# Re-ordering the first stage of a two-block network on one Trainium2 core: operands ahead of squares, eight un-normed blocks in two PSUM groups, modulation weights moved behind the layer norm

## The chip, the core and the metric

The program runs on one core of one Trainium2 chip. The metric is the device time of one execution in microseconds (us). The engines of the core run side by side, each working through its own queue in order: TensorE (PE, matmuls; PEld its weight loads), VectorE (DVE), ScalarE (ACT), GpSimd (POOL) and SyncE (SP), which here only issues transfers from memory. An instruction waits at the head of its engine's queue until what it needs is there, and everything behind it on that engine waits too.

## What is computed

The input x is 512 tokens by 1024 features, in float32. Two network blocks follow each other. The part that the change touches is the first half of the first block:

```python
h = rmsnorm(x, norm1_g)
z = h @ w_in + b_in                       # 1024 -> 6656 columns, 52 blocks of 128
z_glu, z_rx, z_rg, z_ga, z_gb = split(z)
u = z_glu[..., :1024] * sigmoid(z_glu[..., 1024:])
u = causal_depthwise_conv(u, conv_dw_w, conv_dw_b)      # 31 taps
u = silu(layernorm(u, conv_ln_g, conv_ln_b))
y_a = u @ conv_w_out + conv_b_out
xb = causal_depthwise_conv(z_rx, lru_conv_w, lru_conv_b)   # 4 taps
hb = rg_lru(xb, ...)                      # gates of 80 x 80 blocks, a linear recurrence over time
y_b = (hb * gelu(z_rg)) @ lru_w_out
m = sigmoid(z_ga) * y_a + sigmoid(z_gb) * y_b
x = x + m @ w_mix_out
x = x + (silu(h @ ffn_w1) * (h @ ffn_w3)) @ ffn_w2      # h: a second rmsnorm
...
mods = silu(c) @ w_ada + b_ada            # 9 x 1024 numbers, used from the second block on
```

The second block has a feed-forward net, a token mixer (gated linear attention and forgetting attention, merged through w_out) and another feed-forward net; each takes scales and shifts from mods.

## The kernel before

Activations lie transposed: 128 features on the partitions, 512 tokens along the free dimension, so a 1024-wide activation is 8 tiles. A product with a weight block of 1024 x 128 is 8 slices of 128 x 128. For accuracy every operand is split into a rounded high part and a low rest (hi by ScalarE, lo = source - hi by VectorE or GpSimd), and `mm3` (L131 to L134) makes three matmuls of a slice: lines 132, 133, 134. A block of 8 slices is therefore 24 matmuls of 512 columns.

The program is a list of steps. A step has the weight tiles it needs and a function that is called when they are ready. One loop at the end of `build` walks the list, keeps weight transfers and splits (`prep_one`) running ahead, and spends what is left of a step's time, by its own table of costs in us, on a background queue `bg` (`runbg`); `defer(n, f)` calls f some steps later. The calls only name the instructions and their dependences; a scheduler then fixes the order on each engine, and `tc.issue_after(ins)` adds the wish that an instruction stand behind `ins` on its engine.

Staging: a weight tile lands in one of 5 buffers `st`, and its parts go to one of 5 `whi` and 5 `wlo`. Products accumulate in PSUM in one of 3 buffers `mm`; 5 others, `ax`, hold statistics, broadcasts and the convolution's accumulators. A product can begin only when a buffer of its group has been emptied by VectorE or ScalarE.

The order of the work of the first block:

- **Start** (`start_tiles`, L346). For each of the 8 tiles of x: hi and lo of x times the norm's weight g, and the square for the norm's sum. The norm's factor R is not waited for: the first seven blocks (`g0` is two, then `r0` to `r4`) multiply x g, not yet normed, and their results are multiplied by R when they are read (`raw_z`, L391). R takes a column sum over the partitions (ax L196), a square root by Newton steps on VectorE, and a broadcast (dg L217, ax L224).
- **Normed tiles** (`norm_h`, L368): h with R, split, during the un-normed steps. The convolution taps of the un-normed steps wait in the list `late` and are released after the last of these tiles.
- **First stage**, a list of short names (L590): `g` makes a gated unit and queues its 31 convolution taps (VectorE, L406, two accumulators in `ax` in turns, the first tap of each on ScalarE, L401 to L404); `r` makes a tile of z_rx with its 4 taps xb; `a` and `b` are gates, `s` the recurrence, `q` a gelu block times the recurrence, split into hbh and hbl.
- **y_b steps** (`yb_step`, L607): a sigmoid block (thb) and a product of 10 slices over hb.
- **Gate steps** (`ga_step`, L667), then the layer norm of the convolution's output has to be complete (`ln_push`, L651: mean, variance, 1/std, silu and split into u2h and u2l; its sum over tiles, lnm L479, is made by GpSimd), then **y_a steps** (`ya_step`, L676) use it.
- `ada_step` (L316) puts one 128-row piece of w_ada into the list: a transfer of 512 KB and one VectorE product with a sum (L327). 72 of them are spread over the steps: in the y_b steps (every second), the gate steps, six of the y_a steps, and further behind, in w_mix_out, the feed-forward net (`ada_between`: 1.0 a step) and ffn_w2.

`NKEEP` says of which weights tiles may be kept split when a second pass over the tokens' halves reads them again.

## Time and profile before

| | us |
|---|---|
| three runs | 2270.66, 2270.68, 2271.85 (median 2270.68) |
| the profiled execution | 2268.78 |
| its span on the core | 2267.1 |
| TensorE busy in the span | 2207.7 (97%) |
| VectorE busy | 1401.8 (62%) |
| ScalarE busy | 941.8 (42%) |
| GpSimd busy | 159.3 (7%) |

The profiled execution is some 1.7 us longer than its span, which runs from the first to the last instruction. Busy shares are means over stages that differ: in the first 340 us VectorE is busy nearly all the time, later about half. Matmuls are pipelined and overlap, so a matmul's duration in a row (0.4 us for 512 columns) is longer than the distance to the next. An idle piece is shown in brackets behind the instruction that ended it, with what it waited for.

### The profile page before, as it was taken

To read this page: it belongs to the slowest core of one execution; us is meant where nothing else is said; L and a number is where in the kernel's file an instruction comes from. 1 tells how busy PE (TensorE), PEld (TensorE's weight loads), DVE (VectorE), ACT (ScalarE), POOL (GpSimd) and SP (SyncE) were. 2 spreads that over 40 slices of the span, in tenths; PEclk is the share of its full clock that TensorE was granted. 3 is DMA by queue.
4 is the path that set the end of the run, shared out by engine and by line. 5 is a ranking of instruction groups with operands and counts; after the bars stand their busy time and mean duration, and the time that the engine had idled before them with its cause. 6 is when DMAs were issued, how large, how long until landed. Compare 5 with 4: busy or idle time off the path is not lost.

```text
span 2267.1 us, 29984 instructions
## 1 busy us (share of the span) xinstructions
PE 2207.7 (97%) x11688; PEld 1888.2 (83%) x11688; DVE 1401.8 (62%) x2349; ACT 941.8 (42%) x1517; POOL 159.3 (7%) x179
## 2 busy tenths in 40 slices
PE   8899999699999999999999999999999999999997
PEld 6687788588888899988889987888888899988887
DVE  7999996768555448433325768675656558433334
...
GB/s 191 118 92 122 101 134 225 82 144 174 203 195 192 150 103 149 131 94 102 86 102 129 161 96 57 66 47 103 66 75 75 117 89 96 147 95 98 92 121 66
DMA packets 81438, 265.54 MB, mean 117 GB/s; under 512 B 10208, under 2 KB 12512, under 8 KB 81296
## 3 DMA queue, kind: packets, MB, share of 16 engines
...
## 4 chain that ended last, share of the span: by engine, by line
PE 81%; DVE 11%; issue 1%; ACT 1%; DMA 0%; POOL 0%; DVEq 0%; ACTq 0%; POOLq 0%
PE mm L132 24%; PE mm L133 24%; PE mm L134 24%; DVE ax L406 3%; DVE wlo L126 1%; PE ax L1231 1%; PE ax L1232 1%; PE ax L1233 1%; PE ax L1286 1%; PE ax L224 1%; PE ax L1415 1%; DVE xb L406 1%; PE ax L196 1%; DVE xb L567 1%; DMA st<-w_ada 0%
## 5 line engine op out<-in xcount | busy, mean ns | idle before, releaser
L125 ACT ACTIVATE whi<-st 128x1024 fp32r<-128x1024 f32 (+3 forms) x420 | 427.1, 1018 | 959.3 <-PE mm L133 594.4
L126 DVE TENSOR_TENSOR wlo<-st,whi 128x1024 fp32r<-128x1024 f32 (+3 forms) x378 | 454.1, 1202 | 415.8 <-ACT whi L125 414.7
L132 PE MATMUL mm<-pfh,whi 128*128 128x512 f32 (+1 forms) x1676 | 568.9, 339 | 0.5 <-ACT sq L251 0.5
L133 PE MATMUL mm<-pfl,whi 128*128 128x512 f32 (+1 forms) x1676 | 565.6, 338 | 0.0
L134 PE MATMUL mm<-pfh,wlo 128*128 128x512 f32 (+1 forms) x1676 | 564.4, 337 | 1.2 <-DVE wlo L126 1.2
L134 PEld LDWEIGHTS mm<-pfh,wlo 128*128 128x128 f32 x1676 | 316.8, 189 | 34.0 <-DVE wlo L126 1.9
L132 PEld LDWEIGHTS mm<-pfh,whi 128*128 128x128 f32 x1676 | 317.2, 189 | 33.5 <-ACT sq L251 1.4
L133 PEld LDWEIGHTS mm<-pfl,whi 128*128 128x128 f32 x1676 | 317.1, 189 | 31.7 <-issue 0.5
L132 PE MATMUL mm<-hi,whi 128*128 128x512 f32 x464 | 183.0, 394 | 10.4 <-ACT hi L354 6.2
L133 PE MATMUL mm<-lo,whi 128*128 128x512 f32 x464 | 183.4, 395 | 1.3 <-DVE lo L355 1.3
L134 PE MATMUL mm<-hi,wlo 128*128 128x512 f32 x464 | 182.4, 393 | 0.4 <-DVE wlo L126 0.4
L132 PE MATMUL mm<-mh,whi 128*128 128x256 f32 (+1 forms) x528 | 176.7, 335 | 2.2 <-ACT mh L852 1.1
L133 PE MATMUL mm<-ml,whi 128*128 128x256 f32 (+1 forms) x528 | 176.9, 336 | 0.0
L134 PE MATMUL mm<-mh,wlo 128*128 128x256 f32 (+1 forms) x528 | 176.4, 334 | 0.0
L406 DVE SCALAR_TENSOR_TENSOR ax<-th,d_hdw,ax 128x508 f32<-128x508 f32 (+27 forms) x232 | 157.7, 729 | 1.1 <-ACT ax L401 0.2
L133 PE MATMUL mm<-m1l,whi 128*128 128x512 f32 x368 | 143.3, 390 | 0.2 <-DVE m1l L686 0.2
L134 PE MATMUL mm<-m1h,wlo 128*128 128x512 f32 x368 | 143.0, 389 | 0.0
L132 PE MATMUL mm<-m1h,whi 128*128 128x512 f32 x368 | 143.0, 389 | 0.0
L327 DVE SCALAR_TENSOR_TENSOR st<-st,crow 128x1024 f32<-128x1024 f32 x72 | 88.5, 1229 | 73.6 <-DMA st<-w_ada 73.5
L865 DVE TENSOR_TENSOR fs<-fs,mm 128x512 f32<-128x512 f32 (+1 forms) x75 | 45.0, 600 | 128.0 <-PE mm L134 127.7
L132 PEld LDWEIGHTS mm<-hi,whi 128*128 128x128 f32 x464 | 88.1, 190 | 29.6 <-ACT hi L354 6.2
L132 PEld LDWEIGHTS mm<-mh,whi 128*128 128x128 f32 x528 | 100.1, 190 | 13.1 <-ACT mh L852 1.5
...
## 6 DMA issues: line engine op xcount, KB each, us to landing
st<-w_gu SPq DMA_DIRECT2D x102, 512.0 KB, 3.5
st<-w_ada SPq DMA_DIRECT2D x72, 512.0 KB, 4.0
st<-ffn_w SPq DMA_DIRECT2D x56, 512.0 KB, 3.6
st<-w_in SPq DMA_DIRECT2D x51, 512.0 KB, 4.0
st<-w2fm SPq DMA_DIRECT2D x51, 512.0 KB, 3.5
...
st<-w_dn SPq DMA_DIRECT2D x24, 512.0 KB, 3.6
st<-w2v SPq DMA_DIRECT2D x16, 512.0 KB, 3.5
```

Source lines behind the costliest of these rows:

```text
L125: h = act(hi, src, AF.Copy)
L126: (eng or V).tensor_tensor(lo, src, hi, ALU.subtract)
L132: mm(out, whi, xh, start=start, stop=False)
L133: mm(out, whi, xl, start=False, stop=False)
L134: block[0] = mm(out, wlo, xh, start=False, stop=stop)
L196: mm(pc[:, i * nt + j:i * nt + j + 1], acc[:, r[0] + P * j:r[0] + P * (j + 1)], ones1, start=True, stop=True)
L224: mm(R[:, :nt * P], ones, dg.rearrange("p n t -> p (n t)"), start=True, stop=True)
L327: V.scalar_tensor_tensor(w, w, 1.0, crow, ALU.mult, ALU.mult, accum_out=mods[:, n:n + 1])
L406: V.scalar_tensor_tensor(acc[:, d:], u[:, :T - d], w, acc[:, d:], ALU.mult, ALU.add)
L567: V.tensor_tensor_scan(XB[j], GT[0, j], XB[j], 0.0, ALU.mult, ALU.add)
L865: V.tensor_tensor(s, s, rs(st["u"], r), ALU.mult)
L1231: mm(o, h[:, sl], hi[c], start=k == 0, stop=False)
```

## The change

1. **Start.** hi and lo of all eight tiles are made first; the squares follow. The weight tiles of the first four blocks are split at fixed places between them. w_ada and everything else at the start stay where they were.
2. **Un-normed blocks.** `r5` joins them: eight blocks instead of seven. The second, fourth and sixth take an `ax` buffer.
3. **Late list.** After the last normed tile only the first three entries of `late` are released (before: all); the rest, among them the first convolution, is released at the end of the un-normed steps, behind the last of their VectorE reads.
4. **Order wishes.** The first taps and totals of a convolution on ScalarE, and the high parts of xb and hb, are to stand behind the last emptying of a PSUM buffer (`EV`); taps on VectorE behind the last but one of its products (`DV`). The convolution's total overwrites its input instead of a new tile, and the last hb is split one step sooner.
5. **w_ada.** The y_b and gate steps carry none; all eight y_a steps carry one; the feed-forward net takes 1.2 a step; ffn_w2 the rest.
6. **Layer norm.** It is queued one background gap sooner, and the y_b and gate steps spend 1.15 times their rest on the background queue.
7. **NKEEP**: 8 of w_out instead of 3, none of w_mix_out instead of 3.

First place: TensorE's queue from the gate blocks to the y_a blocks (`mm` blocks over hi/lo of h are gate blocks, `ax` rows with ones are column sums, with dg broadcasts, `u2h` is the layer norm's result). Before:

```order
L132 MATMUL mm_3254<-hi_435,whi_3165 128x512
L133 MATMUL mm_3254<-lo_436,whi_3165 128x512
L134 MATMUL mm_3254<-hi_435,wlo_3166 128x512
L196 MATMUL ax_3281<-ones,lnm_1595 128x1 x4
L224 MATMUL ax_3290<-dg_3288,ones 128x512
L196 MATMUL ax_3326<-ones,lnv_3292 128x1 x4
L224 MATMUL ax_3348<-dg_3346,ones 128x512
L132 MATMUL mm_3404<-u2h_3352,whi_3205 128x512
```

With the change:

```order
L134 MATMUL mm_3089<-hi_435,wlo_2961 128x512
L196 MATMUL ax_3116<-ones,lnm_1563 128x1 x4
L132 MATMUL mm_3152<-hi_421,whi_2964 128x512
L133 MATMUL mm_3152<-lo_422,whi_2964 128x512
L134 MATMUL mm_3152<-hi_421,wlo_2965 128x512
L132 MATMUL mm_3152<-hi_423,whi_2964 128x512
L133 MATMUL mm_3152<-lo_424,whi_2964 128x512
L134 MATMUL mm_3152<-hi_423,wlo_2965 128x512
L132 MATMUL mm_3152<-hi_425,whi_2964 128x512
L224 MATMUL ax_3125<-dg_3123,ones 128x512
```

The sums for the mean stood behind the last gate block, and sums and broadcasts of the layer norm without a product between them; now they stand behind the fourth of eight gate blocks, with seven matmuls of the fifth between the sums and the broadcast. The other two steps of the norm have 54 matmuls between this broadcast and the sums of the variance (`lnv`), and 13 between those and their broadcast.

Second place: VectorE's queue at the end of the convolutions (`cv` and `th` with `ax`: a convolution's total; `st,mods`: a w_ada product; `s`, `dg`: the mean). Before:

```order
L327 SCALAR_TENSOR_TENSOR st_3245,mods<-st_3245,crow 128x1024
L126 TENSOR_TENSOR wlo_3206<-st_3129,whi_3205 128x1024
L327 SCALAR_TENSOR_TENSOR st_3303,mods<-st_3303,crow 128x1024
L126 TENSOR_TENSOR wlo_3249<-st_3169,whi_3248 128x1024
L327 SCALAR_TENSOR_TENSOR st_3437,mods<-st_3437,crow 128x1024
L126 TENSOR_TENSOR wlo_3399<-st_3209,whi_3398 128x1024
L327 SCALAR_TENSOR_TENSOR st_3479,mods<-st_3479,crow 128x1024
L126 TENSOR_TENSOR wlo_3441<-st_3252,whi_3440 128x1024
L447 TENSOR_TENSOR cv_3241<-cv_3241,ax_2949 128x512
L634 TENSOR_SCALAR s_3286<-ax_3281 128x4
L217 TENSOR_TENSOR dg_3288<-ident,s_3286 128x512
```

With the change:

```order
L422 SCALAR_TENSOR_TENSOR ax_2859<-th_1676,d_hdw,ax_2859 128x485
L422 SCALAR_TENSOR_TENSOR ax_2858<-th_1676,d_hdw,ax_2858 128x484
L422 SCALAR_TENSOR_TENSOR ax_2859<-th_1676,d_hdw,ax_2859 128x483
L422 SCALAR_TENSOR_TENSOR ax_2858<-th_1676,d_hdw,ax_2858 128x482
L126 TENSOR_TENSOR wlo_3048<-st_2918,whi_3047 128x1024
L475 TENSOR_TENSOR th_1676<-th_1676,ax_2859 128x512
L126 TENSOR_TENSOR wlo_3084<-st_2968,whi_3083 128x1024
L664 TENSOR_SCALAR s_3121<-ax_3116 128x4
L217 TENSOR_TENSOR dg_3123<-ident,s_3121 128x512
L126 TENSOR_TENSOR wlo_3147<-st_2970,whi_3146 128x1024
L669 TENSOR_TENSOR th_319<-th_319,ax_3125 128x512
L669 TENSOR_TENSOR th_705<-th_705,ax_3125 128x512
```

The w_ada products that stood between the wlo rows ahead of the total are gone from here; taps stand in their place.

Third place: ScalarE's queue at the start (`hi`: operands of tile x; `acc`, `sq`: squares; `whi_255`, `whi_159`: weights of the second block, `whi_261`, `whi_179`: of the third). Before:

```order
L354 ACTIVATE hi_138<-x_7_94,pcol 128x512
L251 ACTIVATE sq_173<-x_7_94 128x512
L354 ACTIVATE hi_140<-x_8_95,pcol 128x512
L251 ACTIVATE sq_178<-x_8_95 128x512
L125 ACTIVATE whi_255<-st_118 128x1024
L125 ACTIVATE whi_261<-st_259 128x1024
L361 ACTIVATE R_249<-ax_247 128x512
```

With the change:

```order
L125 ACTIVATE whi_159<-st_118 128x1024
L354 ACTIVATE hi_138<-x_7_94,pcol 128x512
L354 ACTIVATE hi_140<-x_8_95,pcol 128x512
L248 ACTIVATE acc_142<-x_1_88 128x512
L251 ACTIVATE sq_168<-x_2_89 128x512
L251 ACTIVATE sq_171<-x_3_90 128x512
L251 ACTIVATE sq_174<-x_4_91 128x512
L125 ACTIVATE whi_179<-st_177 128x1024
```

The second block's weights moved ahead of the last two operands, the third's behind four of the squares. On TensorE the third block now comes right behind the first; the sums of the squares stand behind its first 19 matmuls, their broadcast five matmuls later, and the second block behind that.

The diff, without blank lines and cut where only context stands:

```diff
@@ -64,7 +64,7 @@
     LA_D, LA_P = 4, 4
-    NKEEP = {"w_mix_out": 3, "w_out": 3, "ffn_w2": 2}
+    NKEEP = {"w_out": 8, "ffn_w2": 2}
     uid = [0]
...
@@ -346,15 +346,24 @@
         acc = at(n="acc")
-        last = H["w0"]
+        H["ha"], H["la"] = H["w0"], None
         for m in range(KT):
...
             g = col("norm1_g", m)
-            with tc.issue_after(last):
-                act(h, X[m], AF.Copy, scale=g)
-            V.scalar_tensor_tensor(l, X[m], g, h, ALU.mult, ALU.subtract)
-            last = sumsq(acc, X[m], FULL, m == 0).ins
-            H["sq", m] = last
+            with tc.issue_after(H["ha"]):
+                H["ha"] = act(h, X[m], AF.Copy, scale=g).ins
+            H["la"] = V.scalar_tensor_tensor(l, X[m], g, h, ALU.mult, ALU.subtract).ins
+            if m in (1, 5):
+                prep_one(0)
+                H["ha"] = H["w1"]
+        for m in range(KT):
+            with tc.issue_after(H["ha"]), tc.issue_after(H["la"]):
+                H["ha"] = sumsq(acc, X[m], FULL, m == 0).ins
+            if m in (3, 7):
+                prep_one(0)
+                H["ha"] = H["w1"]
         derive_all()
...
@@ -363,6 +372,7 @@
+    NEARLY = 3
     late = []
...
@@ -380,19 +390,25 @@
             if m0 + 2 == KT:
-                for f in late:
+                for f in late[:NEARLY]:
                     f()
-                late[:] = [None]
+                del late[:NEARLY]
         return fn
...
         del H["xg"], H["R"]
+        H["h_last"] = H["z_last"]
+        for f in late:
+            f()
+        late[:] = [None]
...
-        ps = pmm()
+        H["nz"] = H.get("nz", 0) + 1
+        ps = pax() if H["nz"] in (2, 4, 6) else pmm()
         gemm(ps, W, H["xg"])
-        V.tensor_tensor(t, ps, H["R"], ALU.mult)
+        H["z_last"] = V.tensor_tensor(t, ps, H["R"], ALU.mult).ins
         return t
...
@@ -407,6 +423,16 @@
     EV = [None]
+    DV = [None, None]
+    def behind_ev():
+        return tc.issue_after(EV[0].ins) if EV[0] is not None else nullcontext()
+    def behind_dv():
+        return tc.issue_after(DV[0].ins) if DV[0] is not None else nullcontext()
+    def dv(ins):
+        DV[:] = [DV[1], ins]
...
@@ -427,8 +453,8 @@
                 gemm(pg, W, H["h"])
-            act(u, pg, AF.Tanh, bias=dcol["hb_in"][:, 8 + m:9 + m], scale=0.5)
-            V.scalar_tensor_tensor(u, u, 1.0, st["a"], ALU.add, ALU.mult)
+            EV[0] = act(u, pg, AF.Tanh, bias=dcol["hb_in"][:, 8 + m:9 + m], scale=0.5)
+            dv(V.scalar_tensor_tensor(u, u, 1.0, st["a"], ALU.add, ALU.mult))
             cv = {}
...
@@ -438,12 +464,14 @@
                         acc = cv["p"][d % 2]
-                        delay(acc, u, d, w, col("conv_dw_b", m), first=d < 2)
+                        with behind_ev() if d < 2 else behind_dv():
+                            delay(acc, u, d, w, col("conv_dw_b", m), first=d < 2)
                 return f
             def total():
-                CV[m] = at(n="cv")
-                act(CV[m], cv["p"][0], AF.Copy)
+                CV[m] = u
+                with behind_ev():
+                    act(u, cv["p"][0], AF.Copy)
                 V.tensor_tensor(CV[m], CV[m], cv["p"][1], ALU.add)
...
@@ -510,7 +538,9 @@
                 XBP[j] = (at(F32R, "xbh"), at(F32R, "xbl"))
-                split(xb, *XBP[j])
+                with behind_ev():
+                    act(XBP[j][0], xb, AF.Copy)
+                V.tensor_tensor(XBP[j][1], xb, XBP[j][0], ALU.subtract)
...
@@ -542,7 +572,7 @@
                 th = at(n="gt")
-                act(th, pg, AF.Tanh, bias=dcol[nmq][:, j:j + 1], scale=0.5)
+                EV[0] = act(th, pg, AF.Tanh, bias=dcol[nmq][:, j:j + 1], scale=0.5)
                 GT[q, j] = th
...
@@ -551,7 +581,7 @@
             V.scalar_tensor_tensor(tt, a2, 1.0, tt, ALU.add, ALU.mult)
-            V.scalar_tensor_tensor(XB[j], ith, 1.0, XB[j], ALU.add, ALU.mult)
+            dv(V.scalar_tensor_tensor(XB[j], ith, 1.0, XB[j], ALU.add, ALU.mult))
             GT[2, j] = tt
...
@@ -578,26 +608,28 @@
             EV[0] = act(ge, pz, AF.Gelu_apprx_tanh, bias=col("b_in", 26 + j))
-            V.tensor_tensor(ge, ge, XB[j], ALU.mult)
+            dv(V.tensor_tensor(ge, ge, XB[j], ALU.mult))
...
                 HB[j] = (at(F32R, "hbh"), at(F32R, "hbl"))
-                split(ge, *HB[j])
-            defer(2, parts)
+                with behind_ev():
+                    act(HB[j][0], ge, AF.Copy)
+                V.tensor_tensor(HB[j][1], ge, HB[j][0], ALU.subtract)
+            defer(2 if j < NRNN - 1 else 1, parts)
         add(wunits("w_in", 26 + j, KT, [8]), fn, own=1.4)
     pool_steps = [0, 0]
-    for it in ("g0 r0 r1 r2 r3 r4 g1 g2 a0 r5 a1 g3 a2 r6 a3 g4 a4 r7 r8 s0 g5 r9 b0 g6 b1 b2 g7 b3 b4 "
+    for it in ("g0 r0 r1 r2 r3 r4 r5 g1 g2 a0 a1 g3 a2 r6 a3 g4 a4 r7 r8 s0 g5 r9 b0 g6 b1 b2 g7 b3 b4 "
                "q0 q1 s1 q2 q3 q4 q5 q6 q7 q8 q9").split():
         n = int(it[1])
-        if it in ("g0", "r0", "r1", "r2", "r3", "r4"):
+        if it in ("g0", "r0", "r1", "r2", "r3", "r4", "r5"):
             {"g": glu_step, "r": rx_step}[it[0]](n, raw=True)
...
                 for m in {"r1": (0, 2), "r2": (4,), "r3": (6,)}[it]:
-                    add([], norm_h(m), own=2.9 + (12.0 if m == 6 else 0.0))
-            if it == "r4":
+                    add([], norm_h(m), own=2.9 + (5.0 if m == 6 else 0.0))
+            if it == "r5":
                 pool_steps[0] = len(steps)
-                add([], raw_end)
+                add([], raw_end, own=8.5)
             continue
...
@@ -611,7 +643,7 @@
             th = at(n="thb")
-            act(th, pz, AF.Tanh, bias=dcol["hb_in"][:, 44 + m:45 + m], scale=0.5)
+            EV[0] = act(th, pz, AF.Tanh, bias=dcol["hb_in"][:, 44 + m:45 + m], scale=0.5)
             st["th"] = th
...
@@ -622,8 +654,6 @@
         add(wunits("lru_w_out", m, NRNN, [5, 5]), fy, own=0.6)
-        if m % 2:
-            ada_step()
...
@@ -649,7 +679,7 @@
     def ln_push(W):
-        bg.extend([NEXT, NEXT])
+        bg.append(NEXT)
         later(0.9, ln_mean)
...
@@ -657,6 +687,7 @@
+    yb0 = len(steps)
     for m in range(KT):
...
@@ -669,9 +700,8 @@
             TA[m] = at(n="tha")
-            act(TA[m], pz, AF.Tanh, bias=dcol["hb_in"][:, 36 + m:37 + m], scale=0.5)
+            EV[0] = act(TA[m], pz, AF.Tanh, bias=dcol["hb_in"][:, 36 + m:37 + m], scale=0.5)
         add(wunits("w_in", 36 + m, KT, [8]), fn)
-        ada_step()
...
@@ -686,8 +716,7 @@
         add(wunits("conv_w_out", m, KT, [8]), fn, own=2.1)
-        if m < 6:
-            ada_step()
+        ada_step()
...
@@ -915,7 +944,7 @@
     def ada_between():
-        H["ada"] = H.get("ada", 0.0) + 1.0
+        H["ada"] = H.get("ada", 0.0) + 1.2
         while H["ada"] >= 1.0:
...
@@ -1565,7 +1594,7 @@
         if 1 <= n <= 5:
-            with tc.issue_after(H["sq", 1] if n == 1 else H["sq", KT - 1] if n < 4 else H["R_last"]):
+            with tc.issue_after(H["ha"] if n < 5 else H["R_last"]):
                 prep_next(step)
...
@@ -1591,8 +1620,8 @@
                 w0 = split(st, hi, lo, G if n in on_pool else None)
-                if n == 0:
-                    H["w0"] = w0.ins
+                if n < 5:
+                    H["w1" if n else "w0"] = w0.ins
                 his += [hi[:, k] for k in range(kc)]
...
@@ -1610,7 +1639,6 @@
     start_tiles()
-    prep_one(0)
     top = 0
...
@@ -1630,7 +1658,7 @@
         elif i < front[0]:
-            runbg(slack - spent[0])
+            runbg((slack - spent[0]) * (1.15 if i >= yb0 else 1.0))
         else:
...
             runbg((slack - prep) * (1.3 if ln_steps[0] <= i < ln_steps[1] else 1.0))
```

## Rows read from the trace of the kernel before

**Rows 1.** Busy time by stretch: each engine's busy us (instructions), clock, DMA share, GB/s.
```profile
core 0: us, PE busy (x) PEld busy (x) DVE busy (x) ACT busy (x) POOL busy (x), PEclk, DMA share, GB/s
60.00:80.00 20.00, 16.25 (x65) 12.97 (x64) 19.92 (x29) 6.19 (x10) 5.26 (x4) 0.91 0.43 110
...
160.00:180.00 20.00, 17.23 (x71) 13.78 (x70) 20.00 (x29) 10.55 (x17) 6.26 (x4) 0.93 0.44 125
...
400.00:420.00 20.00, 5.01 (x12) 2.58 (x12) 15.05 (x33) 5.65 (x9) 0.00 (x0) 0.56 0.08 27
420.00:440.00 20.00, 18.61 (x72) 15.18 (x73) 14.08 (x21) 13.76 (x22) 0.00 (x0) 0.84 0.14 48
...
560.00:580.00 20.00, 20.00 (x90) 16.55 (x89) 10.68 (x16) 5.68 (x8) 0.00 (x0) 1.00 0.71 225
```

**Rows 2.** Timeline of TensorE: start, us, instruction, idle before it and releaser.
```profile
23.62 1.12 PE L224 MATMUL ax<-dg,ones 128*128 128x512 f32 x2
...
67.74 0.73 PE L132 MATMUL mm<-hi,whi 128*128 128x512 f32 x1 [3.75 <-DVE rx L395]
82.00 0.50 PE L132 MATMUL mm<-xbh,whi 128*128 128x512 f32 x1 [1.50 <-ACT th L430]
...
267.40 0.50 PE L133 MATMUL mm<-hbl,whi 128*128 128x512 f32 x1 [2.26 <-DVE hbl L126]
...
398.59 1.05 PE L196 MATMUL ax<-ones,lnm 128*128 128x1 f32 x8 [1.23 <-POOL lnm L479]
400.62 1.13 PE L224 MATMUL ax<-dg,ones 128*128 128x512 f32 x2 [0.98 <-DVE dg L217]
411.40 1.84 PE L196 MATMUL ax<-ones,lnv 128*128 128x1 f32 x8 [9.66 <-DVE lnv L252]
416.49 2.05 PE L224 MATMUL ax<-dg,ones 128*128 128x512 f32 x2 [3.25 <-DVE dg L217]
421.39 1.65 PE L132 MATMUL mm<-u2h,whi 128*128 128x512 f32 x3 [2.85 <-ACT u2h L125]
```

**Rows 3.** Waits of TensorE: releaser, us in total, times, longest.
```profile
PE mm L132 <- ACT ga L421: 5.0, 2, 2.8
```

**Rows 4.** Timeline of VectorE, end of the gate steps.
```profile
379.68 1.23 DVE L327 SCALAR_TENSOR_TENSOR st<-st,crow 128x1024 f32<-128x1024 f32 x1 [2.46 <-DMA st<-w_ada]
...
380.83 1.22 DVE L126 TENSOR_TENSOR wlo<-st,whi 128x1024 fp32r<-128x1024 f32 x1
...
396.44 0.68 DVE L447 TENSOR_TENSOR cv<-cv,ax 128x512 f32<-128x512 f32 x1
```

**Rows 5.** Timeline of VectorE, taps at 56 us and in the y_b steps.
```profile
55.89 11.20 DVE L406 SCALAR_TENSOR_TENSOR xb<-rx,pcol,xb 128x511 f32<-128x511 f32 x12
...
286.85 5.21 DVE L406 SCALAR_TENSOR_TENSOR ax<-th,d_hdw,ax 128x489 f32<-128x489 f32 x8
291.98 1.35 DVE L126 TENSOR_TENSOR wlo<-st,whi 128x640 fp32r<-128x640 f32 x1
293.25 5.36 DVE L406 SCALAR_TENSOR_TENSOR ax<-th,d_hdw,ax 128x500 f32<-128x500 f32 x7
...
299.11 1.89 DVE L126 TENSOR_TENSOR wlo<-st,whi 128x640 fp32r<-128x640 f32 x1
```

**Rows 6.** Groups of GpSimd, 280 to 345 us: busy, mean ns, idle before.
```profile
L126 POOL TENSOR_TENSOR wlo<-st,whi 128x640 fp32r<-128x640 f32 x7 | 12.0, 1716 | 17.4 <-ACT whi L125 17.4
```

**Rows 7.** Tile x, the last two transfers: duration of the issue, starts; landing.
```profile
L340 SPq DMA_DIRECT2D x<-x x2: 430/504/579, 5.6 to 6.3; - x2
...
DMA to landing us min/median/max: 7.3/7.5/7.8
```

**Rows 8.** Timeline of ScalarE and VectorE at the end of the start.
```profile
14.98 0.61 ACT L251 ACTIVATE sq<-x 128x512 f32<-128x512 f32 x1
...
15.50 1.04 ACT L125 ACTIVATE whi<-st 128x1024 fp32r<-128x1024 f32 x1
...
15.91 0.74 DVE L355 SCALAR_TENSOR_TENSOR lo<-x,pcol,hi 128x512 fp32r<-128x512 f32 x1
```

**Rows 9.** DMA issues of the page: count, KB each, median us to landing.
```profile
st<-w_ada SPq DMA_DIRECT2D x72, 512.0 KB, 4.0
```

## The prediction

> **What bounds the kernel now.** I read the busy time by stretch first, then every idle piece of TensorE in the timeline of the first 440 us, then what VectorE did in those places. In a quiet stretch (560 to 580 us) TensorE is never idle and starts 90 matmuls of 512 columns in 20 us, so one costs 0.222 us [rows 1]. The kernel is a queue of matmuls; the time is this queue plus the holes in it. Nearly all holes lie before 440 us [rows 2]: 3.75 us at 64 us (a wait for VectorE's rx, which empties a PSUM buffer), 1.50 us at 80 us and twice ga, 5.0 us together, at 84 and 174 us (ScalarE empties a buffer late) [rows 3], 2.26 us at 265 us (the last hbl), and around the layer norm 1.23, 0.98, 9.66, 3.25 and 2.85 us between 397 and 422 us: 30.5 us. Holes also cost clock. In 60 to 80 us the granted clock is 0.91 and 65 matmuls take 16.25 busy us, 1.8 more than at 0.222; in 160 to 180 us it is 0.93 and 71 take 17.23, 1.45 more; in 400 to 440 us it falls to 0.56 and 0.84, where 72 matmuls take 18.61 (2.6 more) and the second sums and second broadcast take 1.84 and 2.05 against 1.05 and 1.13 of the first: 4.3 more in all [rows 1, 2]. So about 38 us are to be had.
>
> Why is the layer norm late? From 350 to 396 us VectorE has few taps left, but in each gate step it stands about 2.4 us before a w_ada product whose data has not landed, then works 1.2 us on it, then 1.2 us on a wlo; the total of the last convolution, ready long before, comes in this queue only at 396.44 us [rows 4].
>
> **The change part by part.** The two orders hold the same matmuls, and SP issues the same transfers; only w_ada ones move. The new numbers in NKEEP change nothing: w_mix_out's tiles are read once, and of w_out three tiles are kept before and after (the other five are still in their buffers). Cost 0.
>
> *Twelve w_ada products go behind the layer norm, which starts earlier.* On TensorE the sums for the mean stand four blocks (96 matmuls, 21 us) earlier, with gate blocks laid between the steps of the norm. What covers each wait: the 0.98 us before the first broadcast has 7 matmuls (1.55 us); the 9.66 us of variance, plus two wlo of 1.22 us that now stand inside it, 12.1 us, have 54 matmuls (12.0 us); the 3.25 us to the second broadcast have 13 (2.9 us); the 2.85 us to the first u2h have 22 (4.9 us). About 0.5 us stays of these. The condition is that the last convolution is summed in time. Between the last hbl and that total VectorE has 127 taps, 13 wlo, 8 thb and 5 totals. A tap takes 0.641 us where two accumulators take turns (eight from 286.85 to 291.98 us) and 0.77 us where one follows itself (5.36 us for seven) [rows 5]; the new order has only turns here, so 81.4 us; with 13 wlo at 1.22, 13 others at 0.68 and GpSimd's last addition (1.23, the wait before the sums in rows 2) 107.3 us. TensorE has 504 matmuls from the first thb block to the sums for the mean, 112.0 us, less some 3 us in which the last hbl is still made: 109. That is 1.7 us to spare. But eight of the wlo fall among GpSimd's wlo of 1.72 us each [rows 6]; two of 640 columns took 1.35 and 1.89 us there [rows 5], where one of 1024 columns takes 1.22 with GpSimd idle [rows 4]. The bounds are 0 and 8 x 1.72 = 13.7 us; I take 0.5 each, near what the first of those two lost against its size (1.22 x 640/1024 = 0.76), so 4 us, or 2.3 us late, and 2.8 us with the rest of the norm. Of 22.3 us (17.97 idle, 4.3 clock) 19.5 go.
>
> *r5 un-normed, buffers of both groups, the end of the first stage in halves, evacuations first.* From 55.89 us VectorE did twelve taps of xb, 11.2 us [rows 5], ahead of the rx that frees a PSUM buffer; now six stand ahead, and blocks 2, 4 and 6 sit in the other group, so by my count the block that waited finds its buffer free about 2 us before it comes. The 1.50 and 5.0 us of waits were ScalarE evacuations queued behind casts that waited for VectorE taps; now the first convolution starts later and about 40 VectorE instructions fewer (25 us) stand ahead of the first rg product, so those casts are ready. I count 10.2 us idle and 3.25 us clock as gone and give 1 us back for a wait that remains around the first gates: -12.4 us. The taps not done here are those counted above.
>
> *Last hbl:* 47 VectorE instructions fewer ahead of it, and it is split one step sooner: -2.3 us, with no successor, since the product needs it only at its 28th matmul.
>
> *The start.* All eight operands come before the squares. The last x lands at about 14.0 us (issued at 6.2 or 6.3, up to 7.8 to land [rows 7]), so the last hi is there at 14.7 (before, the square behind it began at 14.98) and the last lo, 0.74 us, at 15.5 (before 16.65) [rows 8], and block 0 ends 1.2 us earlier, at 16.0. Then TensorE's queue holds not the second block, whose weights are ready, but the third (whi_179), whose cast stands behind four squares: 14.7 + 4 x 0.52 + 1.0 = 17.8 [rows 8], its wlo 19.1, 17 further matmuls to 22.8; then the sums (1.05, to 23.9), five matmuls, and the broadcast only after the square-root chain of 3.25 us [rows 2] at 27.1, over at 28.3. Before, the broadcast at 23.62 us ended at 24.7 [rows 2] and TensorE had as many matmuls done 1.1 us later, at 25.9. So the start costs 2.4 us; bounds -1.2 (the gain of block 0 alone) and +4. R is about 3 us later; the next block that waits for what hangs on it is the one at 64 us, and the 2 us counted there are with R late.
>
> *w_ada at 1.2 per FFN step instead of 1.0, and 12 of 12 in ffn_w2.* Before, an FFN step of 5.33 us carried one weight tile and one w_ada with VectorE busy 10.68 of 20 us and TensorE full [rows 1]. A fifth more adds 0.25 us of VectorE and takes the transfers from 197 (two tiles of 0.52 MB in 5.33 us) to 216 GB/s, below the 225 of that row: 0; at most +5, a few such stands of 2.46 us [rows 4].
>
> Sum: 2268.8 (the profiled execution) + 2.4 - 12.4 - 2.3 - 19.5 = 2237.0 us. That execution lay 1.9 us under the median of the runs (2270.7); on that scale it is 2238.9. I predict 2238.
>
> *A rule weighed.* Row: the two wlo on VectorE among GpSimd's were 0.6 and 1.1 us longer than their size asks [rows 5]. The Trainium skill's page "SBUF — State Buffer", section "Who interferes with whom", says that VectorE with two SBUF inputs and GpSimd reading SBUF lock each other out for a whole instruction. By that rule each of the eight wlo could wait for all of a GpSimd one; the trace so far shows part of it. It is the first rival below, priced from rows.
>
> **Rivals.**
> 1. *VectorE does not finish the last convolution in time.* Each wlo waits a whole GpSimd wlo: 13.7 us instead of 4, so TensorE stands 12 us at the sums for the mean, with another 2.5 us of clock. For it: VectorE has 1.7 us to spare in 109, and every wlo of 8 that loses more than 0.2 us is felt. Against: waits of that length are the longest seen. Time 2238 - 2 + 12 + 2.5 = 2250 (half of it: 2244).
> 2. *The y_a weights starve.* Four w_ada tiles sit in the five staging buffers until the norm ends, so a weight tile passes alone: 4.0 us to land, as a w_ada tile of the same size does [rows 9], 1.0 cast, 1.22 wlo, 6.2 us against 5.33 a block; 0.9 x 8 = 7 us: 2245. Against: three of these tiles are ready before the norm ends, and the order leaves 20 matmuls between the fourth and its use.
> 3. *Slower.* In the FFN each w_ada product makes VectorE stand before its data as in the gate steps. Per step: 1.2 x (wait + 1.23) + 1.22 + 0.6 must stay under 5.33 us; 38 steps lie there, and the gain of 32 us is eaten when a step takes 6.2 us, that is from a wait of 2.4 us each. With 2.9 us each a step takes 6.8 us: 38 x 1.45 = 55 us, or 2293. For it: the wait in the gate steps is 2.46 [rows 4]. Against: there VectorE had nothing else to do and TensorE never waited; with one w_ada a step the FFN shows no hole.
> 4. *The moved work does not move TensorE:* the early holes come back at other buffers (13 us), only the norm's gain stays: 2252.
>
> **Chances.** Forecast 0.66; rival 1 0.16; rival 2 0.06; rival 3 0.03; rival 4 0.09. The forecast's own range is 2231 (the start gains 1.2, nothing is late, 1 us fewer left) to 2244; with half of the others 2229 to 2252. What a measurement of this kernel can tell from no change is about 0.2% (4.5 us): faster 0.95, within 0.02, slower 0.03.
>
> **What would show it.** In the new profile: the hole of 9.66 us is under 1 us and the slices between 380 and 440 us have a granted clock of 1.00; the first wait for rx at 64 us and the hbl one are gone; w_ada rows of VectorE first appear after u2l; TensorE waits 1.5 to 3 us for dg at about 25 us. Wrong: a wait of 5 us or more for lnm (rival 1), waits for wlo in the y_a blocks (2), or any new idle time after 450 us (3).

## The result, and the profile after

The changed kernel takes 2243.1 us (four runs, 2240.97 to 2243.89) against 2271.3 for the kernel before on the same chip: a ratio of 0.9874, interval 0.9857 to 0.9891, or 28 us less. Forecast were 2238 us and a range of 2229 to 2252. The profiled execution took 2240.97 us, its span 2239.3.

Both traces hold 11,688 matmuls of TensorE, so the time by which the n-th starts earlier than before can be read off as a ledger. It shows where the time came from, stage by stage:

```
matmul no.  starts before  starts after  gained so far  what lies between
   100          35.27         38.79          -3.5        start, R
   250          74.91         72.79          +2.1        hole for rx, with its clock
   300          90.53         84.12          +6.4        holes for th and ga
   400         113.20        110.12          +3.1        a new hole at 89 us
   700         186.56        178.47          +8.1        small hole, ga with its clock
  1050         268.44        257.80         +10.6        last hbl
  1650         426.49        394.31         +32.2        layer norm
  1900         483.73        453.89         +29.8        new holes at the first products of w_mix_out
  9600        1890.82       1862.43        +28.4        the clock at 1853 us
  last        2258.07       2229.96        +28.1
```

The stretches that answer to [rows 1], by the same columns, from the kernel after:

```profile
20.00:40.00 20.00, 18.11 (x75) 13.93 (x74) 12.26 (x24) 7.16 (x9) 2.68 (x5) 0.91 0.42 140
60.00:80.00 20.00, 20.00 (x90) 16.57 (x89) 16.59 (x23) 9.89 (x16) 7.59 (x5) 1.00 0.19 54
160.00:180.00 20.00, 19.97 (x88) 16.22 (x87) 20.00 (x30) 14.74 (x24) 10.06 (x7) 1.00 0.57 177
400.00:420.00 20.00, 20.00 (x90) 16.57 (x89) 18.34 (x27) 8.32 (x11) 0.00 (x0) 1.00 0.85 274
420.00:440.00 20.00, 19.35 (x86) 15.69 (x84) 17.04 (x26) 7.88 (x12) 0.00 (x0) 1.00 0.74 251
```

Where 12 and 72 matmuls stood between 400 and 440 us there are 90 and 86, at full clock (1.00). The lower clock (0.91) is now in the second stretch of the start. TensorE's timeline (start, duration, instruction, idle time before it and its releaser) at the places of [rows 2]:

```profile
16.93 0.50 PE L132 MATMUL mm<-hi,whi 128*128 128x512 f32 x1 [1.13 <-ACT whi L125]
18.41 0.50 PE L134 MATMUL mm<-hi,wlo 128*128 128x512 f32 x1 [0.75 <-DVE wlo L126]
26.63 1.60 PE L224 MATMUL ax<-dg,ones 128*128 128x512 f32 x2 [1.89 <-DVE dg L217]
...
89.49 0.47 PE L132 MATMUL mm<-xnh,whi 128*128 128x512 f32 x1 [2.21 <-DMA xnh<-xbh]
90.52 0.47 PE L133 MATMUL mm<-xnl,whi 128*128 128x512 f32 x1 [0.56 <-DMA xnl<-xbl]
...
364.79 0.95 PE L196 MATMUL ax<-ones,lnm 128*128 128x1 f32 x8
367.31 1.02 PE L224 MATMUL ax<-dg,ones 128*128 128x512 f32 x2
380.48 1.05 PE L196 MATMUL ax<-ones,lnv 128*128 128x1 f32 x8
384.69 1.12 PE L224 MATMUL ax<-dg,ones 128*128 128x512 f32 x2
...
440.25 0.49 PE L132 MATMUL mm<-m1h,whi 128*128 128x512 f32 x1 [0.89 <-ACT m1h L715]
441.32 0.50 PE L133 MATMUL mm<-m1l,whi 128*128 128x512 f32 x1 [0.58 <-DVE m1l L716]
443.31 0.73 PE L132 MATMUL mm<-m1h,whi 128*128 128x512 f32 x2 [0.56 <-ACT m1h L715]
```

The four steps of the norm carry no bracket any more: TensorE waits for none of them. What is new are the hole at the edge tiles of the gates (xnh, xnl: the half tiles that neighbouring gate blocks share, moved by SyncE's transfers at L556) and three small ones at 440 us. None stands in [rows 2].

### The profile page after: what moved, and what is told of

Its sections match the earlier page's. It is cut to its first block, busy times and chain, and to the rows that moved or that the text cites. A ratio compares the mean times of both kernels' runs of the same rounds, so it can differ in the third digit from the quotient of the medians.

```text
span 2239.3 us, 29970 instructions
## 1 busy us (share of the span) xinstructions
PE 2203.3 (98%) x11688; PEld 1886.5 (84%) x11688; DVE 1402.1 (63%) x2350; ACT 940.7 (42%) x1517; POOL 164.2 (7%) x179
## 3 DMA queue, kind: packets, MB, share of 16 engines
q8 instruction: 92, 1.51, 0.3%
## 4 chain that ended last, share of the span: by engine, by line
PE 91%; DVE 5%; ACT 2%; DMA 2%; issue 1%; SPq 0%; DVEq 0%; ACTq 0%
PE mm L132 27%; PE mm L133 27%; PE mm L134 27%; PE ax L1260 1%; PE ax L1261 1%; PE ax L1262 1%; DVE wlo L126 1%; PE ax L1315 1%; PE ax L224 1%; PE ax L1444 1%; PE ax L196 1%; DMA x<-x 1%; PE ax L133 0%; PE ax L134 0%; PE ax L132 0%
## 5 line engine op out<-in xcount | busy, mean ns | idle before, releaser
L126 DVE TENSOR_TENSOR wlo<-st,whi 128x1024 fp32r<-128x1024 f32 (+2 forms) x378 | 454.1, 1202 | 368.9 <-ACT whi L125 368.1
L133 PEld LDWEIGHTS mm<-pfl,whi 128*128 128x128 f32 x1676 | 317.1, 189 | 31.8 <-issue 0.5
L132 PE MATMUL mm<-hi,whi 128*128 128x512 f32 x440 | 172.8, 393 | 7.3 <-ACT hi L354 6.2
L133 PE MATMUL mm<-lo,whi 128*128 128x512 f32 x440 | 173.7, 395 | 0.5 <-DVE lo L355 0.5
L134 PE MATMUL mm<-hi,wlo 128*128 128x512 f32 x440 | 172.9, 393 | 0.7 <-DVE wlo L126 0.7
L422 DVE SCALAR_TENSOR_TENSOR ax<-th,d_hdw,ax 128x510 f32<-128x510 f32 (+28 forms) x232 | 154.4, 730 | 0.0
L133 PEld LDWEIGHTS mm<-ml,whi 128*128 128x128 f32 x528 | 100.8, 191 | 10.3 <-DVE ml L882 0.2
```

What stands on the lines that cost most here:

```text
L126: (eng or V).tensor_tensor(lo, src, hi, ALU.subtract)
L132: mm(out, whi, xh, start=start, stop=False)
L133: mm(out, whi, xl, start=False, stop=False)
L134: block[0] = mm(out, wlo, xh, start=False, stop=stop)
L422: V.scalar_tensor_tensor(acc[:, d:], u[:, :T - d], w, acc[:, d:], ALU.mult, ALU.add)
```

## The experiments

Each version is compared with the kernel before, run on the same chip beside it. "At matmul 400" and the like compare the start of the same matmul with the profile of the changed kernel.

**1. The w_ada pieces moved, with the norm's place on the background queue.** The kernel before with these edits and no other part of the change:

```diff
-        if m % 2:
-            ada_step()          # y_b steps
-        ada_step()              # gate steps
-        if m < 6:
-            ada_step()          # y_a steps
+        ada_step()
-        H["ada"] = H.get("ada", 0.0) + 1.0
+        H["ada"] = H.get("ada", 0.0) + 1.2
-        bg.extend([NEXT, NEXT])
+        bg.append(NEXT)
-            runbg(slack - spent[0])
+            runbg((slack - spent[0]) * (1.15 if i >= yb0 else 1.0))
```

> The kernel before with one part of the change: no w_ada piece in the y_b and gate steps, one in each y_a step, 1.2 instead of 1.0 a step in the feed-forward net, and the background queue of the layer norm run as in the change. Theory A (the norm was late because VectorE stood behind w_ada in its queue): all of the norm's gain is here, about 21 us at the first u2h, of which 2 to 4 us go again at the start of w_mix_out, where y_a now carries two pieces more: 2252 us, within 2249 to 2255; the early holes (64, 82, 86, 177, 267 us) stay as before. Theory B (the norm needs the re-ordered first stage and taps too, since the last convolution is late otherwise): TensorE waits 3 us or more for lnm and the time is 2256 to 2266.

2254.7 us, ratio 0.9919 (0.9905 to 0.9934). The early holes are all there. From matmul 1300 to 1650 it loses 2.9 us against the change, where the kernel before loses 21.5: 18.7 of the 21.5 us of the norm come from this part alone. That w_ada's place is needed for it is shown by version 2; what the two edits of the background queue add was not separated. There is no wait for lnm; the holes left are 0.41 us (lnv) and 1.70 and 0.65 us (u2h, u2l). Theory A, but for its last part: at the first products of w_mix_out it waits 0.23 us, no more than the kernel before, though its y_a steps carry the same eight pieces as in the change.

**2. The w_ada pieces put back into the change** (the first three edits above reversed, and 1.0 a step).

> The changed kernel with the w_ada pieces back where they were (every second y_b step, all gate steps, six y_a steps, 1.0 a step in the feed-forward net); the rest of the change stays. Theory A: the holes between the sums for the mean and the first u2h come back, 10 us or more in total with the clock falling there, less the 2.4 us of w_mix_out that go: 2252 to 2266 us. Theory B (it is the order of gate blocks and taps that covers the norm): those holes stay under 3 us and the time is 2238 to 2244.

2258.4 us, ratio 0.9939 (0.9924 to 0.9954): 17.8 us lost against the change from matmul 1050 to 1650. The blocks still lie between the steps of the norm, but one wait is 12.79 us, and the granted clock is at its lower level (1.2 GHz; 0.50 from 395 to 411 us) for 17 us. TensorE's timeline of this version:

```profile
370.19 1.05 PE L196 MATMUL ax<-ones,lnm 128*128 128x1 f32 x8 [0.63 <-POOL lnm L507]
...
390.25 0.95 PE L196 MATMUL ax<-ones,lnv 128*128 128x1 f32 x8
403.99 2.07 PE L224 MATMUL ax<-dg,ones 128*128 128x512 f32 x2 [12.79 <-DVE dg L217]
408.91 1.65 PE L132 MATMUL mm<-u2h,whi 128*128 128x512 f32 x3 [2.85 <-ACT u2h L125]
```

VectorE's timeline says why: the square-root chain is a dozen steps of 0.16 us, and between most of them now stands a w_ada product of 1.22 us or a wlo. The chain takes from 391.23 to 403.9 us; in the change it takes from 381.57 to 384.6.

```profile
393.66 0.17 DVE L207 TENSOR_SCALAR s<-s 128x4 int32<-128x4 int32 x1
393.73 1.22 DVE L327 SCALAR_TENSOR_TENSOR st<-st,crow 128x1024 f32<-128x1024 f32 x1
...
394.87 0.16 DVE L200 TENSOR_TENSOR s<-s 128x4 f32<-128x4 f32 x1
394.94 1.22 DVE L327 SCALAR_TENSOR_TENSOR st<-st,crow 128x1024 f32<-128x1024 f32 x1
```

**3. The second un-normed block in the first group**, so that TensorE has it right behind the first block (in TensorE's order the sums then stand behind 59 matmuls of products and the broadcast behind 72; in the change behind 43 and 48).

```diff
-        ps = pax() if H["nz"] in (2, 4, 6) else pmm()
+        ps = pax() if H["nz"] in (4, 6) else pmm()
```

> The changed kernel with only the fourth and sixth un-normed block in the other PSUM group, so that the second block, whose weights are ready, comes right behind the first on TensorE. Theory A (the start loses 3.5 us because TensorE's queue holds the third block, whose weights are cast behind the squares, and then the broadcast with 5 matmuls of cover): the holes at 16.9, 18.4 and 26.6 us and the drop of the clock at 27 us go; matmul 100 stands 4 to 5 us earlier than in the change, the time is 2238 to 2240 (about 4 us faster). Theory B (R is late in any case, and with three blocks in the first group the fourth or fifth waits for it): a hole of 2 us or more appears between 30 and 45 us and the gain is under 2 us.

2241.8 us, ratio 0.9862 (0.9846 to 0.9879), not to be told from the change. But the start does what was said: the holes at 17, 18 and 27 us and the drop of the clock there are gone, matmul 100 is 6.9 us earlier. The gain is then lost again: 2.2 us at 63 us, and the rest at the edge tiles, which TensorE gets only 1.4 us earlier than in the change.

```profile
62.76 0.50 PE L132 MATMUL mm<-hi,whi 128*128 128x512 f32 x1 [2.19 <-DVE rx L411]
88.08 0.77 PE L132 MATMUL mm<-xnh,whi 128*128 128x512 f32 x1 [5.22 <-DMA xnh<-xbh]
```

Both theories were wrong about the place: neither had the edge tiles.

**4. All eight un-normed blocks in the first group** (`in ()` in the same line).

> The changed kernel with all eight un-normed blocks in the first PSUM group. As in the version with the second block there, the start is 6.9 us earlier at matmul 100. Theory A (two groups are what removed the hole of 3.75 us for rx): with three buffers for eight blocks the fourth block waits for R at 27 us and the hole at 55 to 65 us is 3 us or more; at matmul 250 the kernel is level with the change or later, time 2242 to 2246. Theory B (r5 un-normed and the taps in two halves removed it): holes for PSUM before 65 us of 2.5 us at most in total, as where only the second block went back; time 2240 to 2243, what is left of the start being lost at the edge tiles at 88 us.

2241.2 us, ratio 0.9861 (0.9845 to 0.9878), again not to be told from the change. One wait for R is left, 1.41 us at 29 us, and no hole for rx at all: at matmul 250 it is 5.1 us ahead of the change. So the second group is not what removed the hole of 3.75 us (theory B; which of its two parts did, r5 or the taps in two halves, was not separated), and it costs the start 5 us. At 87 us the edge tiles take these 5 us back (a wait of 4.92 us): the change hid its own start loss behind them.

**5. No wishes for order behind evacuations and products.** `behind_ev()` and `behind_dv()` return `nullcontext()`.

> The changed kernel without the wishes that a cast or a first tap stand behind the last evacuation and a tap behind the last of VectorE's products (EV and DV): TensorE's order is the same, ScalarE and VectorE go back to the scheduler's own. Theory A (the 6.5 us of waits for th and ga at 82, 86 and 177 us, with 1.5 us of clock, went because evacuations stand first): waits for ga, th or gt of 1.5 us or more come back, at least 4 us in total, time 2246 to 2250. Theory B, the one of the prediction (they went because some 40 VectorE instructions fewer stand ahead of the first rg product, so that the casts are ready in any order): less than 1.5 us comes back, time 2241 to 2244.

2260.6 us, ratio 0.9944 (0.993 to 0.9959): 19 us of profile lost, 4.1 by matmul 400, 6.8 more by 700, 8.3 more at the last hbl by 1300. Two waits for ga are back, longer than before, 10.2 us together:

```profile
90.33 0.79 PE L132 MATMUL mm<-xbh,whi 128*128 128x512 f32 x1 [5.35 <-ACT ga L447]
```
```profile
179.04 0.80 PE L132 MATMUL mm<-xbh,whi 128*128 128x512 f32 x1 [4.86 <-ACT ga L447]
```

ScalarE's timeline of this version shows the cause. At 89 us the first tap of a convolution (L417, L420) stands ahead of the evacuation ga (L447), and waits 7.18 us for a product (th, L457) that VectorE reaches only behind its taps; at 177 us it is a cast (xbh, L542), which waits 11.18 us for VectorE's taps:

```profile
87.56 0.78 ACT L417 ACTIVATE ax<-th,pcol,d_hdw 128x512 f32<-128x512 f32 x1 [7.18 <-DVE th L457]
...
88.47 0.69 ACT L420 ACTIVATE ax<-th,d_hdw 128x511 f32<-128x511 f32 x1
89.09 0.61 ACT L125 ACTIVATE whi<-st 128x512 fp32r<-128x512 f32 x1
89.61 0.67 ACT L447 ACTIVATE ga<-mm,pcol 128x512 f32<-128x512 f32 x1
...
176.84 0.63 ACT L542 ACTIVATE xbh<-xb 128x512 fp32r<-128x512 f32 x1 [11.18 <-DVE xb L422]
...
178.32 0.67 ACT L447 ACTIVATE ga<-mm,pcol 128x512 f32<-128x512 f32 x1
```

Theory A, and more than it asked for. What the prediction saw, evacuations behind work that waits for VectorE, is there; that fewer VectorE instructions ahead would make the casts ready is refuted. The edit takes away both kinds of wishes that the change adds, on ScalarE and on VectorE; how much belongs to each was not separated.

**6. Two wlo from GpSimd to VectorE.** In the change GpSimd makes two wlo from 77 to 86 us, in 6.40 and 2.86 us (4.6 on average), where one takes 2.4 to 2.6 elsewhere; VectorE's xbl in that stretch take 2.24 us for 0.68.

```diff
-            on_pool.update(n for n in ids if n % 3 != 2)
+            on_pool.update(n for n in ids if n % 3 != 2 and n not in (15, 16))
```

> The changed kernel with two weight tiles (the two whose low parts GpSimd makes from 77.0 to 86.3 us, 4.6 us each where one takes 2.4 alone) split on VectorE instead. Theory A (the new hole of 2.77 us at 89 us, 3.3 with the clock, comes from GpSimd and VectorE shutting each other out: the staging buffers come free late, SyncE stands before its next weight load until 83.5 us, and the transfers of the gates' edge tiles xnh and xnl are queued behind it): SyncE issues them 3 us or more earlier, the hole falls under 1 us, the low parts of xb on VectorE fall from 2.24 to 0.68 us, and the time falls by 2.5 to 3.5 us. Theory B (the operands xb themselves are late, since the taps of the un-normed blocks are released only after r5): the hole stays at 2 us or more, time within 1 us of the change.

2240.7 us, ratio 0.9864 (0.9849 to 0.9878), not to be told from the change as a whole. GpSimd's and VectorE's timelines, of the change

```profile
77.04 6.40 POOL L126 TENSOR_TENSOR wlo<-st,whi 128x1024 fp32r<-128x1024 f32 x1 [3.96 <-ACT whi L125]
83.40 2.86 POOL L126 TENSOR_TENSOR wlo<-st,whi 128x1024 fp32r<-128x1024 f32 x1
...
81.75 2.24 DVE L543 TENSOR_TENSOR xbl<-xb,xbh 128x512 fp32r<-128x512 f32 x1
83.91 0.74 DVE L422 SCALAR_TENSOR_TENSOR ax<-th,d_hdw,ax 128x509 f32<-128x509 f32 x1
84.56 2.24 DVE L543 TENSOR_TENSOR xbl<-xb,xbh 128x512 fp32r<-128x512 f32 x1
```

and VectorE's of this version:

```profile
83.81 0.68 DVE L543 TENSOR_TENSOR xbl<-xb,xbh 128x512 fp32r<-128x512 f32 x1
84.42 0.74 DVE L422 SCALAR_TENSOR_TENSOR ax<-th,d_hdw,ax 128x510 f32<-128x510 f32 x1
85.07 0.68 DVE L543 TENSOR_TENSOR xbl<-xb,xbh 128x512 fp32r<-128x512 f32 x1
```

The times of the change fit turns. Up to 81.17 us VectorE has instructions with two operands in SBUF without a break (taps of xb, a wlo, an xbl), and GpSimd's first wlo ends 2.2 us behind them; the xbl that begins at 81.75 us ends 0.6 us behind that wlo, at 83.99, and the next one 0.5 us behind the second wlo. The taps between them read their accumulator from PSUM and keep their 0.74 us. SyncE stands for the first wlo, as its waits of 79 to 84 us show, and issues the next weight load at 83.47 us, 0.07 us after its end:

```profile
SPq L1590 <- POOL wlo L126: 2.5, 1, 2.5
```

In this version the xbl are as fast as expected, the wait for xnh falls from 2.21 to 0.83 us (0.54 stays for xnl), and from matmul 300 to 400 the version gains 1.4 us on the change: half of theory A. SyncE issues the edge transfers only 1.1 us earlier against TensorE's matmuls, and still just behind a weight load, which now waits 1.3 us for VectorE's wlo.

**7. The edge transfers issued by ScalarE** (`nc.scalar.dma_start` for `nc.sync.dma_start` at L556).

> The changed kernel with the transfers of the edge tiles xnh and xnl issued by ScalarE's queue instead of SyncE's. Theory A1 (what delays them is their place in SyncE's queue behind the weight loads, and their landing 5 us later behind these): they are issued when xbl is there, 1 to 2.5 us earlier, land in 2 to 3 us, the hole at 89 us goes, time 2.5 to 3.5 us less than the change, unless ScalarE, which now waits for VectorE's xbl at each of them, is late with an evacuation (then a new hole of 1 to 2 us before 110 us). Theory B (the operands are late): the hole stays at 2 us or more.

2252.6 us, ratio 0.9916 (0.9901 to 0.9931). The transfer that was late is issued at 81.75 us and lands at 84.07; no wait for xnh is left. But ScalarE issues in order too. From 84 to 96 us it only issues edge transfers or stands before them, and the evacuation ga comes 10 us late:

```profile
96.80 0.79 PE L132 MATMUL mm<-xbh,whi 128*128 128x512 f32 x1 [9.97 <-ACT ga L447]
```

The condition in the expectation decided, with 10 us where 1 to 2 were named, and not for the reason that it gives: the last xbl of this stretch is made at 89.65 us, but ScalarE's issues of 85.93, 90.67 and 92.29 us come right behind the landing of three of SyncE's weight loads (85.86, 90.64 and 92.27 us), which the trace names as their releasers.

**8. w_ada in six y_a steps, 1.3 a step in the feed-forward net.**

```diff
-        ada_step()
+        if m < 6:
+            ada_step()
-        H["ada"] = H.get("ada", 0.0) + 1.2
+        H["ada"] = H.get("ada", 0.0) + 1.3
```

> The changed kernel with a w_ada piece in the first six y_a steps only, as before, and 1.3 instead of 1.2 a step in the feed-forward net. Theory A (the three holes of 0.89, 0.58 and 0.56 us at the first products of w_mix_out come from VectorE standing before the last two w_ada pieces in y_a): they go, but for 0.2 us, and the time falls by 2 to 2.4 us to 2240.5 to 2241.5. Theory B (they come from the y_a steps being nearer together, or from pieces still queued from the norm): 1.5 us or more of holes stay, time 2242 to 2244. In the feed-forward net neither theory expects a hole; one would mean that 1.3 a step is too many.

2247.2 us, ratio 0.9888 (0.9874 to 0.9903). At 441 us 0.54 us of holes are left of 2.03, and 2 us are gained by matmul 1850. In the feed-forward net 6.3 us are then lost between matmuls 2600 and 3000. TensorE's waits of this version from 500 to 780 us (us in total, times, longest; the change has none there):

```profile
PE mm L132 <- DVE fs L895: 4.7, 5, 1.5
```

VectorE's timeline there has w_ada products that waited 0.6 to 3.8 us for their data, with fs, which empties a PSUM buffer, behind some of them.

```profile
669.37 1.23 DVE L327 SCALAR_TENSOR_TENSOR st<-st,crow 128x1024 f32<-128x1024 f32 x1 [3.42 <-DMA st<-w_ada]
...
670.52 0.69 DVE L895 TENSOR_TENSOR fs<-fs,mm 128x512 f32<-128x512 f32 x1
```

The prediction's third rival, which it gave 0.03, is real and begins between 1.2 and 1.3 pieces a step, with 6 us where 55 were priced. VectorE's stands alone do not make it: from 500 to 780 us they add up to 94.0 us here and to 94.9 in the change, where TensorE waits for none of them (43.7 in the kernel before). Why fs comes late at 1.3 and not at 1.2 is not shown.

**9. Edits 3 and 6 together, with w_ada in six y_a steps and six (for four) w_mix_out steps.**

> The changed kernel with three edits together: the second un-normed block in the first PSUM group, the two weight tiles of 77 us split on VectorE, and w_ada in the first six y_a steps and six w_mix_out steps (1.2 in the feed-forward net stays). By theory A: the start gives back 6.9 us at matmul 100; the hole for rx at 63 us keeps 2.5 of it; with the edge tiles in time the rest is no longer lost at 89 us; at w_mix_out 2 us of holes go: 5.5 to 8 us less than the change, 2235 to 2238. By theory B (edge tiles late through their operands): 2239 to 2241, with a hole of 3 us or more at 85 to 90 us. Neither expects a hole in the feed-forward net.

2237.7 us, ratio 0.9852 (0.9836 to 0.9869), the profile 5.4 us under the change. With the edge tiles earlier (waits of 1.29 and 0.57 us) 4.7 us of the start's gain stay at matmul 400. The holes at w_mix_out stay (0.68 and 1.09 us): the last m1l now stands behind a w_ada product that waits 1.11 us for its data at 436 us.

**10. The same, with the edge transfers called a step earlier**, ahead of two weight loads in SyncE's queue:

```diff
-                defer(3, lambda m=m: sides(m))
+                defer(2, lambda m=m: sides(m))
```

> The version of three edits (second block in the first group, two weight tiles on VectorE, w_ada spread to w_mix_out) and the edge transfers called one step earlier, so that in SyncE's queue two weight loads that stood ahead of 14 of them stand behind. Theory A2 (what is left of the wait at 85 us, 1.29 and 0.57 us, is the landing, 4.7 us behind a weight load issued 0.4 us before, where it was 2.3 us in the kernel before): they land 2.3 to 3 us after issue, no wait for xnh is left; 2 to 3 us less than the version of three: 0.984 to 0.9845 of the kernel before. Theory B (SyncE then stands before xbl, and the weight loads behind it come late): a new wait of TensorE for whi or wlo of 1 us or more between 85 and 110 us, and the time is the same or longer.

2236.2 us, ratio 0.9843 (0.9828 to 0.9858), the lowest, but not to be told from version 9: both profiles have a span of 2233.8 us. The change once more on that chip is at 2242.3. Landing, of the change and then of this version, in the view of tile xnh:

```profile
DMA to landing us min/median/max: 2.4/4.5/5.1
```
```profile
DMA to landing us min/median/max: 2.2/2.3/2.3
```

No wait for the edge tiles is left. One of 1.64 us for an evacuation (th) at 81 us comes in its place, so that 0.9 us are gained on version 9 at matmul 400 and not 2 to 3. At the first products of w_mix_out they are lost again, with holes of 2.6 us where version 9 has 1.8.

**11. Version 9 with the eighth un-normed block in the second group** (`in (4, 6, 8)`).

> The version of three edits with the fourth, sixth and eighth un-normed block in the other PSUM group (there the fourth and sixth alone). Theory A (the 2.2 us for rx at 63 us are a buffer of the first group, held by the block three allocations earlier until VectorE reads it): the block that waits now takes a buffer released two blocks earlier, the wait goes; but the edge tiles at 85 us, which do not depend on TensorE, come no earlier, so that all but 0.5 us of it is lost there: within 1 us of the version of three, hole at the edge tiles 3.5 us or more. Theory B (VectorE's work is pulled forward with it): edge tiles 2 us earlier too, time 2 us less.

2239.2 us, ratio 0.9855 (0.9838 to 0.9871). The hole for rx goes; 1.97 us for the low part of a normed tile (lo, L391) at 57 us and 1.12 for th at 81 stand in its place, and at matmul 400 it is 0.3 us ahead of version 9. The hole of 3.5 us at the edge tiles did not come. It then loses 6.1 us at w_mix_out, where the clock falls too (holes of 2.17 and 1.17 us).

**12. The change once more.**

> The changed kernel once more, unaltered, beside the versions that follow: 27 to 29 us less than the kernel before, 0.987 to 0.988 of it, with the same holes at 17 to 18, 27, 89 and 440 us. In the profiles so far one or two drops of the clock of 3.4 us each (1.7 us of time) fell at different places in kernels with the same holes, so the span may differ by 2 us from the first one.

2242.3 us, ratio 0.9873 (0.9858 to 0.9887). The holes are the same to 0.7 us. The clock falls at 1854 us as in the first profile, but at the start at 18 us, for twice as long, and not at 27 us.

## Why the prediction was right, and where it was not

**The total.** Forecast for the profiled execution were 2237.0 us, measured 2240.97: a gain of 31.8 against 27.8.

**The layer norm: -19.5 forecast, -21.5 measured** (matmuls 1050 to 1650). Mechanism and condition held, and both directions of the test (1, 2) confirm it. The term left 2.3 us for a late last convolution; there was none, but by little. GpSimd's last addition ends at 364.45 us, and the sums begin at 364.79:

```profile
362.31 2.14 POOL L507 TENSOR_TENSOR lnm<-lnm,th 128x512 f32<-128x512 f32 x1 [27.80 <-DVE th L475]
```

Both sides of the race were mis-sized. From the last hbl (249.92 us) to the end of this addition it took 114.5 us, against 111.3 forecast. From the same hbl to the sums TensorE gave 114.9 us, against 109. Of these 5.9 us, 2.3 are the matmul: 504 were set at 0.222 us each, from 90 in 20 us, but that row counts every matmul that reaches into the stretch, and only 88 begin there; 50 of them in an undisturbed stretch take 11.33 us in either trace, 0.2267 each. The other 3.6 are the last hbl, for which 3 us were taken off: the 504 matmuls begin with the first product over hb, at 250.54 us, and it was ready 0.6 us before that. That the cover was the more mis-sized of the two is luck.

The first rival's mechanism is there without its price. Four of the thirteen wlo that VectorE makes in this stretch took 1.94 us for 1.22, each beginning 0.42 us behind an addition of GpSimd; the other nine met nothing.

```profile
258.98 1.29 POOL L507 TENSOR_TENSOR lnm<-lnm,th 128x512 f32<-128x512 f32 x1 [6.06 <-DVE th L475]
...
259.40 1.94 DVE L126 TENSOR_TENSOR wlo<-st,whi 128x1024 fp32r<-128x1024 f32 x1
```

By the rule of the Trainium skill's page "SBUF — State Buffer", section "Who interferes with whom", each could have waited for a whole GpSimd instruction. The trace agrees with the rule, here and in 6, but what was left to wait for was the rest of an addition, 0.72 us each.

**The early holes: -12.4 forecast, -11.6 measured** (matmuls 100 to 1000). The sum is near, but two of its reasons fell, so that its nearness is in part luck. The hole for rx went, but not through the buffers of the other group (4). The waits for th and ga went through the order behind evacuations, not because "about 40 VectorE instructions fewer" make the casts ready (5): without the wishes these matmuls gain less than 0.5 us on the kernel before. The wishes were costed at nothing as a step of their own, and without them the change gains 11.9 us, not 28. And the new hole at 89 us, 3.3 us with its slow matmuls, was not seen: 14.9 us went, 3.3 came. It is the fourth rival in part, in a place that the prediction did not look at. Versions 6, 7 and 10 show what it is made of: a wlo of GpSimd that VectorE's work holds up for 4 us, the weight load that waits for its staging buffer, and transfers queued behind that load.

**The last hbl: -2.3 forecast, -2.6 measured.** Its reason was fewer instructions ahead and an earlier split; version 5 has both and loses 8.3 us against the change here (after matmul 700), so the order behind evacuations is needed as well.

**The start: +2.4 forecast, +3.5 measured.** The three waits came where the order of TensorE and ScalarE said; in the trace of after the broadcast waits 1.89 us for dg at 26.6 us, in the 1.5 to 3 that were named. What was left out is the clock: after this idle piece the granted clock falls, and matmuls 57 to 64 start up to 1.2 us apart. In the second profile of the change (12), where the clock fell earlier and for longer, the start costs 5.2 us. This loss set nothing: versions 3 and 4 take it away and the time does not move, since TensorE then waits for the edge tiles instead (5.22 and 4.92 us).

**w_ada behind the norm: 0 forecast, +2.4 measured.** The failed step is that the part of the sum on w_ada spoke of the feed-forward net alone, where indeed no wait came, and not of what waits for VectorE at the end of y_a. It is the second rival's mechanism with another victim. SyncE's timeline of after, while the norm runs and behind it, and its longest wait there:

```profile
386.36 0.33 SPq L1590 DMA_DIRECT2D st<-conv_w_out  x1
399.76 0.33 SPq L1590 DMA_DIRECT2D st<-w_ada  x1
```

```profile
SPq L1590 <- DVE st L327: 13.0, 1, 13.0
```

For 13.4 us it issues nothing, since the staging buffers hold w_ada pieces that VectorE takes up only at the end of its u2l, from 398.5 us on. Everything then comes at once (274 GB/s in the row of 400 to 420 us). Up to w_mix_out's first product VectorE makes twelve pieces, the eight of y_a and the four of the w_mix_out steps, which stand among the ya tiles too. The last of the twelve still waits for its data, with the sixth of the eight ya tiles behind it on VectorE:

```profile
433.23 1.23 DVE L327 SCALAR_TENSOR_TENSOR st<-st,crow 128x1024 f32<-128x1024 f32 x1 [0.82 <-DMA st<-w_ada]
434.38 0.08 DVE L327 DVE_READ_ACCUMULATOR st<-st,crow 128x1 f32 x1
434.38 0.69 DVE L712 SCALAR_TENSOR_TENSOR ya<-tha,ya 128x512 f32<-128x512 f32 x1
```

So the last m1h and m1l are late. With two pieces fewer 0.54 us of holes are left of 2.03 (8); with two fewer in y_a and two more in the w_mix_out steps 1.77 stay (9). Version 1 has the same twelve and 0.23 us, but four of them are done by 384 us, ahead of the norm. So the holes go with the number of pieces between the norm and w_mix_out, whichever steps carry them: twelve in the change and in 9, ten in 8, eight in 1. What the held buffers add was not separated.

**The rest.** The 1.5 us at 1853 us belong to no part of the change: after the same idle pieces (0.84 and 1.11 us) the granted clock fell in this execution and not in the one of before; it fell near there in eleven of the fourteen profiles taken, and two of the three without it (4 and 6) are versions of the change.
